# RMSNorm over 16384 rows: row scales on ScalarE, gamma from PSUM in bulk on VectorE, part of the rows on GpSimd, third tile stored in halves, gamma loaded in five pieces

## Chip, cores, metric

One core of one Trainium2 chip. The metric is device time of one execution in microseconds (us), median over runs. The kernel before takes 161.9 us (three runs, 161.73 to 162.24).

In the lines of the profile DVE is VectorE, ACT ScalarE, POOL GpSimd, PE TensorE, and SP the engine that issues the transfers of x; SPq is SP's queue of such issues. L101 is line 101 of the kernel file of that run. SBUF and PSUM are the two on-chip memories; a tile called slot lies in SBUF. A queue "runs dry" when all transfers issued so far are done. The "slack" of a store is the time by which its first byte could move before the transfers ahead of it are through.

## The reference

```python
def reference(x, gamma):                    # x: 16 x 1024 x 512 f32, gamma: 512 f32
    rms = np.sqrt(np.mean(x ** 2, axis=-1, keepdims=True) + 1e-5)
    return (x / rms * gamma).astype(np.float32)
```

33.5 MB come in and 33.5 MB go out. There is very little arithmetic for each byte.

## The kernel before

The 16384 rows are cut into four tiles of 128 partitions x 32 rows x 512. In this text a "row" is one 128x512 slice of a tile, 0.26 MB; a tile has 32 of them. There are three buffers of 64 KB per partition; tile 3 reuses the buffer of tile 0, so its load waits for tile 0's store. All transfers of x are issued by SP, in order, on one queue.

```python
load(0, 0, 0, 8)                       # tile, buffer, first row, last row
load(0, 0, 8, 32)
...
def row_stats(slot, g):                # 8 rows at a time
    if (g // G) % 2:                   # every other group: squares into PSUM, summed on VectorE
        for h in range(0, G, H):
            nc.scalar.activation(out=sq, in_=slots[slot][:, g+h : g+h+H, :], func=AF.Square)
            nc.vector.tensor_reduce(out=ss[:, h : h+H], in_=sq, axis=mybir.AxisListType.X, op=OP.add)
    else:                              # the others: ScalarE squares and sums row by row
        for r in range(G):
            nc.scalar.activation(out=sq_scratch, in_=slots[slot][:, g+r, :], func=AF.Square,
                                 accum_out=ss[:, r : r+1])
    nc.scalar.activation(out=rms, in_=ss, func=AF.Sqrt, bias=eps_t, scale=1.0 / D)
    nc.vector.reciprocal(out=rstd, in_=rms)

def apply(slot, g, rstd):              # x * rstd * gamma, one VectorE instruction per row
    for r in range(G):
        nc.vector.scalar_tensor_tensor(out=slots[slot][:, g+r, :], in0=slots[slot][:, g+r, :],
            scalar=rstd[:, r : r+1], in1=gamma_b, op0=OP.mult, op1=OP.mult)

def transfers(t, g):                   # issued by SP after apply() of group (t, g)
    if (t, g) == (0, 0):
        store(0, 0, 0, 1); load(1, 1, 0, 32); load(2, 2, 0, 16); store(0, 0, 1, 2); load(2, 2, 16, 32)
    elif (t, g) == (0, 24):
        store(0, 0, 2, 16); store(0, 0, 16, 32); load(3, 0, 0, 16); load(3, 0, 16, 32)
    elif (t, g) == (1, 24): store(1, 1, 0, 32)
    elif (t, g) == (2, 24): store(2, 2, 0, 32)
    elif (t, g) == (3, 8):  store(3, 0, 0, 16)
    elif (t, g) == (3, 24): store(3, 0, 16, 32)
```

## Time and profile before

| | before |
|---|---|
| time | 161.9 us |
| span of the profiled run | 160.4 us |
| x's DMA queue, share of 16 engines' span | 97.7% |
| busy: VectorE, ScalarE, GpSimd | 122.6, 80.1, 0.2 us |

All data go over one queue, and its transfers fill the 16 DMA engines for 97.7% of the span. The lines and their reading are in the prediction.

### The profile page before, as it was taken

The page shows a single profiled execution, that of the slowest core. Times are in us where ns is not written, and L with a number is a line of the kernel's source. Part 1 is how long each engine was busy: PE and PEld are TensorE (multiplying, and loading weights), DVE is VectorE, ACT ScalarE, POOL GpSimd, SP SyncE. Part 2 cuts the span into 40 slices and gives each one's busy share as a digit, 9 for nine tenths or more (in the row PEclk, how much of TensorE's full clock was granted, in tenths as well). Part 3 has the DMA queues.
Part 4 walks back from the last instruction along what each step waited for, and adds up shares of the span by engine and source line. Part 5 has one row for each costly group of instructions (what it writes and reads, how often), then busy time and mean ns, then how long its engine had stood idle before and what let it go on. Part 6 is the DMA issues. An engine that isn't in the chain of part 4 may idle for free.

```text
span 160.4 us, 410 instructions
## 1 busy us (share of the span) xinstructions
PE 2.0 (1%) x2; PEld 0.5 (0%) x2; DVE 122.6 (76%) x163; ACT 80.1 (50%) x162; POOL 0.2 (0%) x4
## 2 busy tenths in 40 slices
PE   4000000000000000000000000000000000000000
PEld 1000000000000000000000000000000000000000
DVE  0100928999999519999999999999999999994000
ACT  3098039990390999996900950079609940000000
POOL 0000000000000000000000000000000000000000
DMA  5999999699699999999999999998998998999993
GB/s 197 523 392 392 466 449 523 261 523 523 262 402 387 455 458 418 453 415 466 409 392 498 409 400 507 409 507 376 425 507 360 441 507 360 417 400 441 449 417 147
DMA packets 2164, 67.13 MB, mean 419 GB/s; under 512 B 241, under 2 KB 241, under 8 KB 498
## 3 DMA queue, kind: packets, MB, share of 16 engines
q1 hardware_dynamic: 2160, 67.11, 97.7%
q14 instruction: 2, 0.02, 0.0%
q10 hardware_dynamic: 2, 0.00, 0.0%
HBM read 33.56 MB, written 33.55 MB: 418 GB/s over the span
## 4 chain that ended last, share of the span: by engine, by line
DVE 67%; DMA 13%; ACT 7%; issue 2%; DVEq 0%; SPq 0%
DVE slot L88 48%; DVE ss L71 18%; DMA slot<-in_x_dram 13%; ACT sq_scratch L76 3%; ACT sq L70 3%; DVE rstd L83 1%; DVEq L154 0%; ACT rms L82 0%; SPq L42 0%
## 5 line engine op out<-in xcount | busy, mean ns | idle before, releaser
L88 DVE SCALAR_TENSOR_TENSOR slot<-slot,rstd,gamma_b 128x512 f32<-128x512 f32 x128 | 85.8, 738 | 0.1
L76 ACT ACTIVATE sq_scratch<-slot 128x512 f32<-128x512 f32 x64 | 40.0, 625 | 10.0 <-DMA slot<-in_x_dram 8.7
L70 ACT ACTIVATE sq<-slot 128x2048 f32<-128x2048 f32 x16 | 29.8, 1864 | 18.6 <-DVE ss L71 11.5
L71 DVE TENSOR_REDUCE ss<-sq 128x4 f32<-128x2048 f32 x16 | 35.9, 2274 | 3.4 <-ACT sq L70 3.4
L82 ACT ACTIVATE rms<-ss,eps_t 128x8 f32<-128x8 f32 x16 | 4.6, 297 | 25.9 <-DVE ss L71 25.7
L83 DVE RECIPROCAL rstd<-rms 128x8 f32<-128x8 f32 x16 | 3.1, 193 | 16.1 <-ACT rms L82 16.1
L76 ACT ACTIVATION_READ_ACCUMULATOR sq_scratch<-slot 128x1 f32 x64 | 11.9, 186 | 0.0
L57 DVE COPY gamma_b<-sq 128x512 f32<-128x512 f32 x1 | 0.7, 691 | 3.3 <-PE sq L55 3.3
L55 PE MATMUL sq<-gamma_row,ones_col 1*128 1x512 f32 x2 | 2.0, 1122 | 2.2 <-DMA gamma_row<-in_gamma_dram 2.2
L76 ACT ACT_TABLE_LOAD x1 | 1.3, 1283 | 1.3 <-PEq L143 1.3
L82 ACT ACT_TABLE_LOAD x1 | 1.3, 1283 | 0.0
L53 DVE MEMSET ones_col<- 1x128 f32 x1 | 0.2, 165 | 0.8 <-PEq L143 0.8
L55 PEld LDWEIGHTS sq<-gamma_row,ones_col 1*128 1x128 f32 x2 | 0.5, 306 | 2.2 <-issue 2.2
L143 POOL MEMSET const-bfloat16-1.0<- 128x1 bf16 x1 | 0.1, 101 | 0.0
L143 POOL MEMSET const-uint8-127<- 128x1 uint8 x1 | 0.1, 101 | 0.0
L143 POOL MEMSET const-float32-0.0<- 128x1 f32 x1 | 0.1, 98 | 0.2 <-issue 0.2
L143 POOL MEMSET const-float32-1.0<- 128x1 f32 x1 | 0.1, 98 | 0.0
L60 DVE MEMSET eps_t<- 128x1 f32 x1 | 0.1, 59 | 0.0
## 6 DMA issues: line engine op xcount, KB each, us to landing
slot<-in_x_dram SPq DMA_DIRECT2D x4, 4096.0 KB, 27.6
out_dram<-slot SPq DMA_DIRECT2D x3, 4096.0 KB, 18.8
slot<-in_x_dram SPq DMA_DIRECT2D x1, 6144.0 KB, 21.5
out_dram<-slot SPq DMA_DIRECT2D x1, 3584.0 KB
slot<-in_x_dram SPq DMA_DIRECT2D x1, 2048.0 KB, 7.2
out_dram<-slot SPq DMA_DIRECT2D x2, 256.0 KB, 21.3
out_dram<-slot SPq DMA_DIRECT2D x2, 29.8
gamma_row<-in_gamma_dram ACTq DMA_DIRECT2D x1, 2.0 KB
```

Source lines behind the costliest of these rows:

```text
L53: nc.vector.memset(ones_col, 1.0)
L55: nc.tensor.matmul(gamma_psum[:, 0], ones_col, gamma_row, start=True, stop=True)
L57: nc.vector.tensor_copy(out=gamma_b, in_=gamma_psum[:, 0])
L60: nc.vector.memset(eps_t, eps)
L70: nc.scalar.activation(out=sq, in_=slots[slot][:, g + h : g + h + H, :], func=AF.Square)
L71: nc.vector.tensor_reduce(out=ss[:, h : h + H], in_=sq, axis=mybir.AxisListType.X, op=OP.add)
L76: nc.scalar.activation(out=sq_scratch, in_=slots[slot][:, g + r, :], func=AF.Square, accum_out=ss[:, r : r + 1],)
L82: nc.scalar.activation(out=rms, in_=ss, func=AF.Sqrt, bias=eps_t, scale=1.0 / D)
L83: nc.vector.reciprocal(out=rstd, in_=rms)
L88: nc.vector.scalar_tensor_tensor(out=slots[slot][:, g + r, :], in0=slots[slot][:, g + r, :], scalar=rstd[:, r : r + 1], in1=gamma_b, op0=O ...
L143: nc = _bacc.Bacc("TRN2", target_bir_lowering=False, num_devices=1)
```

## The change

The change takes work off VectorE: each row was one VectorE instruction with two SBUF inputs. Now 7 or 8 rows of a group of 16 (3 at the two ends) go to GpSimd, in two passes (times the row's scale, then times gamma). ScalarE scales the others by row; VectorE multiplies these by gamma in bulk and takes gamma from PSUM. VectorE also sums the squares of all rows now. The transfers are nearly the same: tile 1's load is issued up front, tile 2 is stored in two halves, and some of the loads and stores of tiles 0 and 2 are cut smaller. The core of the diff (bookkeeping of dependences, pools and comments cut):

```diff
     load(0, 0, 0, 8)
-    load(0, 0, 8, 32)
+    load(0, 0, 8, 16)
+    load(0, 0, 16, 32)
+    load(1, 1, 0, 32)
...
-    nc.scalar.dma_start(out=gamma_row, in_=gamma.unsqueeze(0))
+    pieces = (0, 128, 224, 320, 416, D)
+    for c0, c1 in zip(pieces, pieces[1:]):
+        nc.scalar.dma_start(out=gamma_row[:, c0:c1], in_=gamma.unsqueeze(0)[:, c0:c1])
...
+    groups = [                          # tile, first row, rows, pieces squared at once, GpSimd's share
+        (0, 0, 8, (4, 4), 3), (0, 8, 8, (4, 4), 3), (0, 16, 16, (7, 5, 4), 7),
+        (1, 0, 16, (7, 5, 4), 8), (1, 16, 16, (7, 5, 4), 8), (2, 0, 16, (7, 5, 4), 8),
+        (2, 16, 16, (7, 5, 4), 7), (3, 0, 16, (7, 5, 4), 7), (3, 16, 16, (7, 5, 4), 3),
+    ]
...
+    def scale_by_pool(rstd, t, g, n, share):
+        nc.gpsimd.tensor_tensor(out=part, in0=part, in1=by_row, op=OP.mult)
+        last = nc.gpsimd.tensor_tensor(out=part, in0=part, in1=gamma_b.to_broadcast([P, share, D]), op=OP.mult)
+    def scale_rows(rstd, t, g, r0, r1):
+        for r in range(r0, r1):
+            nc.scalar.activation(out=x[:, g + r, :], in_=x[:, g + r, :], func=AF.Copy, scale=rstd[:, r])
+        scaled = nc.vector.tensor_tensor(out=part, in0=part, in1=gamma_psum.to_broadcast([P, r1 - r0, D]), op=OP.mult)
...
-        elif (t, g) == (2, 24):
-            store(2, 2, 0, 32)
+        elif (t, g) == (2, 0):
+            store(2, 2, 0, 16)
+        elif (t, g) == (2, 16):
+            store(2, 2, 16, 32)
```

The order in the loop: for group k, GpSimd's two passes are issued first, then the squares of group k+1 (12 of its 16 rows), half of group k's row scales, the rest of the squares, the other half, and at last the square root and reciprocal of group k+1.

More of the change, by code (lines that the diff above doesn't have):

```diff
@@ L27 @@
     R = 32
-    G = 8
-    H = 4
     assert N == 4 * P * R
@@ L33 @@
     ov = of.rearrange("(t p r) d -> t p r d", p=P, r=R)
+    ctx.enter_context(tc.manual_schedule())
+    nc.scalar.addr_align(128, offset=0, max_nops=0)
     const = ctx.enter_context(tc.tile_pool(name="const", bufs=1))
-    stats = ctx.enter_context(tc.tile_pool(name="stats", bufs=4))
-    psum = ctx.enter_context(tc.tile_pool(name="psum", bufs=2, space=bass.MemoryType.PSUM))
+    stats = ctx.enter_context(tc.tile_pool(name="stats", bufs=9))
+    psum = ctx.enter_context(tc.tile_pool(name="psum", bufs=1, space=bass.MemoryType.PSUM))
@@ L39 @@
     slots = [const.tile([P, R, D], fp32, name=f"slot{i}") for i in range(3)]
+    before_scale = []
     def load(t, slot, r0, r1):
-        nc.sync.dma_start(out=slots[slot][:, r0:r1], in_=xv[t][:, r0:r1])
+        dma = nc.sync.dma_start(out=slots[slot][:, r0:r1], in_=xv[t][:, r0:r1])
+        before_scale.append((slot, r0, r1, dma))
     def store(t, slot, r0, r1):
-        nc.sync.dma_start(out=ov[t][:, r0:r1], in_=slots[slot][:, r0:r1])
+        dma = nc.sync.dma_start(out=ov[t][:, r0:r1], in_=slots[slot][:, r0:r1])
+        before_scale.append((slot, r0, r1, dma))
@@ L47 @@
     load(0, 0, 0, 8)
-    load(0, 0, 8, 32)
+    load(0, 0, 8, 16)
+    load(0, 0, 16, 32)
+    load(1, 1, 0, 32)
     gamma_row = const.tile([1, D], fp32)
-    nc.scalar.dma_start(out=gamma_row, in_=gamma.unsqueeze(0))
+    pieces = (0, 128, 224, 320, 416, D)
+    for c0, c1 in zip(pieces, pieces[1:]):
+        nc.scalar.dma_start(out=gamma_row[:, c0:c1], in_=gamma.unsqueeze(0)[:, c0:c1])
     ones_col = const.tile([1, P], fp32)
-    nc.vector.memset(ones_col, 1.0)
-    gamma_psum = psum.tile([P, H, D], fp32, name="sq")
+    nc.gpsimd.memset(ones_col, 1.0)
@@ L55 @@
+    gamma_psum = psum.tile([P, 1, D], fp32, name="gamma_psum")
     nc.tensor.matmul(gamma_psum[:, 0], ones_col, gamma_row, start=True, stop=True)
-    gamma_b = const.tile([P, D], fp32)
-    nc.vector.tensor_copy(out=gamma_b, in_=gamma_psum[:, 0])
+    gamma_b = const.tile([P, 1, D], fp32)
     eps_t = const.tile([P, 1], fp32)
-    nc.vector.memset(eps_t, eps)
-    sq_scratch = const.tile([P, D], fp32)
-    def row_stats(slot, g):
-        ss = stats.tile([P, G], fp32, name="ss")
-        rms = stats.tile([P, G], fp32, name="rms")
-        rstd = stats.tile([P, G], fp32, name="rstd")
-        if (g // G) % 2:
-            for h in range(0, G, H):
-                sq = psum.tile([P, H, D], fp32, name="sq")
-                nc.scalar.activation(out=sq, in_=slots[slot][:, g + h : g + h + H, :], func=AF.Square)
-                nc.vector.tensor_reduce(
-                    out=ss[:, h : h + H], in_=sq, axis=mybir.AxisListType.X, op=OP.add
-                )
-        else:
-            for r in range(G):
-                nc.scalar.activation(
-                    out=sq_scratch,
-                    in_=slots[slot][:, g + r, :],
-                    func=AF.Square,
-                    accum_out=ss[:, r : r + 1],
-                )
-        nc.scalar.activation(out=rms, in_=ss, func=AF.Sqrt, bias=eps_t, scale=1.0 / D)
-        nc.vector.reciprocal(out=rstd, in_=rms)
-        return rstd
@@ L86, in apply @@
-    def apply(slot, g, rstd):
-        for r in range(G):
-            nc.vector.scalar_tensor_tensor(
-                out=slots[slot][:, g + r, :],
-                in0=slots[slot][:, g + r, :],
-                scalar=rstd[:, r : r + 1],
-                in1=gamma_b,
-                op0=OP.mult,
-                op1=OP.mult,
-            )
-    groups = [(t, g) for t in range(4) for g in range(0, R, G)]
-    slot_of = [0, 1, 2, 0]
+    nc.gpsimd.memset(eps_t, eps)
+    groups = [
+        (0, 0, 8, (4, 4), 3),
+        (0, 8, 8, (4, 4), 3),
+        (0, 16, 16, (7, 5, 4), 7),
+        (1, 0, 16, (7, 5, 4), 8),
+        (1, 16, 16, (7, 5, 4), 8),
+        (2, 0, 16, (7, 5, 4), 8),
+        (2, 16, 16, (7, 5, 4), 7),
+        (3, 0, 16, (7, 5, 4), 7),
+        (3, 16, 16, (7, 5, 4), 3),
+    ]
@@ new lines, with square_sums, inverse_rms @@
+    slot_of = [0, 1, 2, 0]
+    def square_sums(ss, t, g, r, m, k):
+        home, name, most = ((psum, "sq_psum", 7), (const, "sq_sbuf", 5))[k % 2]
+        sq = home.tile([P, most, D], fp32, name=name)
+        rows = slots[slot_of[t]][:, g + r : g + r + m, :]
+        nc.scalar.activation(out=sq[:, :m], in_=rows, func=AF.Square)
+        nc.vector.tensor_reduce(
+            out=ss[:, r : r + m, 0], in_=sq[:, :m], axis=mybir.AxisListType.X, op=OP.add
+        )
+    def inverse_rms(ss, n):
+        nc.scalar.activation(out=ss[:, :n, 0], in_=ss[:, :n, 0], func=AF.Sqrt, bias=eps_t, scale=1.0 / D)
+        nc.vector.reciprocal(out=ss[:, :n, 0], in_=ss[:, :n, 0])
+        return ss
@@ new lines, in scale_by_pool @@
+    def scale_by_pool(rstd, t, g, n, share):
+        part = slots[slot_of[t]][:, g + n - share : g + n, :]
+        by_row = rstd[:, n - share : n].to_broadcast([P, share, D])
+        nc.gpsimd.tensor_tensor(out=part, in0=part, in1=by_row, op=OP.mult)
+        last = nc.gpsimd.tensor_tensor(
+            out=part, in0=part, in1=gamma_b.to_broadcast([P, share, D]), op=OP.mult
+        )
+        before_scale.append((slot_of[t], g + n - share, g + n, last))
+    def scale_rows(rstd, t, g, r0, r1):
+        x = slots[slot_of[t]]
+        for r in range(r0, r1):
+            nc.scalar.activation(out=x[:, g + r, :], in_=x[:, g + r, :], func=AF.Copy, scale=rstd[:, r])
+        part = x[:, g + r0 : g + r1, :]
+        scaled = nc.vector.tensor_tensor(out=part, in0=part, in1=gamma_psum.to_broadcast([P, r1 - r0, D]), op=OP.mult)
+        for slot, b0, b1, earlier in before_scale:
+            if slot == slot_of[t] and b0 < g + r1 and g + r0 < b1:
+                tc.declare_no_dep(scaled.ins, earlier.ins, reason="ScalarE waited for it before it scaled these rows")
@@ L102, in transfers @@
             store(0, 0, 0, 1)
-            load(1, 1, 0, 32)
             load(2, 2, 0, 16)
             store(0, 0, 1, 2)
-            load(2, 2, 16, 32)
-        elif (t, g) == (0, 24):
-            store(0, 0, 2, 16)
+            load(2, 2, 16, 24)
+            store(0, 0, 2, 3)
+            load(2, 2, 24, 32)
+        elif (t, g) == (0, 16):
+            store(0, 0, 3, 16)
             store(0, 0, 16, 32)
@@ L111, in transfers, with pieces_of @@
             load(3, 0, 16, 32)
-        elif (t, g) == (1, 24):
+        elif (t, g) == (1, 16):
             store(1, 1, 0, 32)
-        elif (t, g) == (2, 24):
-            store(2, 2, 0, 32)
-        elif (t, g) == (3, 8):
+        elif (t, g) == (2, 0):
+            store(2, 2, 0, 16)
+        elif (t, g) == (2, 16):
+            store(2, 2, 16, 32)
+        elif (t, g) == (3, 0):
             store(3, 0, 0, 16)
-        elif (t, g) == (3, 24):
+        elif (t, g) == (3, 16):
             store(3, 0, 16, 32)
-    ahead = row_stats(0, 0)
-    for k, (t, g) in enumerate(groups):
-        rstd = ahead
-        if k + 1 < len(groups):
-            tn, gn = groups[k + 1]
-            ahead = row_stats(slot_of[tn], gn)
-        apply(slot_of[t], g, rstd)
+    def pieces_of(group):
+        t, g, n, pieces, share = group
+        ss = stats.tile([P, 16, 1], fp32, name="ss")
+        r = 0
+        todo = []
+        for k, m in enumerate(pieces):
+            todo.append((ss, t, g, r, m, k))
+            r += m
+        return ss, todo
+    ss, todo = pieces_of(groups[0])
+    for piece in todo:
+        square_sums(*piece)
+    rstd = inverse_rms(ss, groups[0][2])
+    nc.scalar.copy(out=gamma_b[:, 0], in_=gamma_psum[:, 0])
+    for k, group in enumerate(groups):
+        t, g, n, pieces, share = group
+        mine = n - share
+        half = (mine + 1) // 2
+        ahead = groups[k + 1 :][:1]
+        ss, todo = pieces_of(ahead[0]) if ahead else (None, [])
+        scale_by_pool(rstd, t, g, n, share)
+        for piece in todo[:2]:
+            square_sums(*piece)
+        if n < 16:
+            scale_rows(rstd, t, g, 0, mine)
+        else:
+            scale_rows(rstd, t, g, 0, half)
+        for piece in todo[2:]:
+            square_sums(*piece)
+        if n == 16:
+            scale_rows(rstd, t, g, half, mine)
         transfers(t, g)
+        for nxt in ahead:
+            rstd = inverse_rms(ss, nxt[2])
 _INS = ['x', 'gamma']
```

## The prediction

> **What bounds the kernel now.** I read the page first: the engines, the 40 slices, the DMA queues and the chain that ended last; then the issues of the SP queue and the end of DVE's timeline; then the busy time in three stretches.
>
> The page of the kernel before:
>
> ```profile
> PE 2.0 (1%) x2; PEld 0.5 (0%) x2; DVE 122.6 (76%) x163; ACT 80.1 (50%) x162; POOL 0.2 (0%) x4
> ...
> DMA  5999999699699999999999999998998998999993
> ...
> q1 hardware_dynamic: 2160, 67.11, 97.7%
> ...
> DVE 67%; DMA 13%; ACT 7%; issue 2%; DVEq 0%; SPq 0%
> ```
>
> The last line tempts one to call the kernel DVE-bound. The one above it decides otherwise: q1, which carries all loads and stores, kept the 16 DMA engines busy for 97.7% of 160.4 us, 156.7 us. The chain only says who issued the last store, not whether the DMA would have had something else to do meanwhile. The windows show the same (columns: us from the span's start, length, busy time and instructions per engine, PE clock, DMA share, GB/s):
>
> ```profile
> 1.70:20.00 18.30, 2.04 (x2) 0.50 (x2) 5.03 (x9) 8.22 (x19) 0.00 (x0) 1.00 1.01 423
> 20.00:140.00 120.00, 0.00 (x0) 0.00 (x0) 111.15 (x144) 71.43 (x143) 0.00 (x0) 1.00 1.00 431
> 140.00:159.20 19.20, 0.00 (x0) 0.00 (x0) 6.23 (x10) 0.00 (x0) 0.00 (x0) 1.00 0.93 401
> ```
>
> DMA share 1.00 at 431 GB/s for 120 us: no hole to fill. The packet records in the trace put the first descriptor of q1 at 1.74 us and the last end at 159.25, so 157.5 us carry 256 rows in and out (a row here is 128x512 f32, 0.26 MB): 0.615 us a row. What is not transfer is 1.74 us ahead and 1.15 us behind, which both kernels have.
>
> Compute runs ahead of the queue. The last issues and the last DVE work:
>
> ```profile
> 85.63 60.96 SPq L45 DMA_DIRECT2D out_dram<-slot  x4
> ...
> 136.26 9.97 DVE L88 SCALAR_TENSOR_TENSOR slot<-slot,rstd,gamma_b 128x512 f32<-128x512 f32 x15
> ```
>
> The fourth of these stores is issued when DVE ends, 146.2 us. Its 16 rows come after 240 others, so the queue needs it only at 1.74 + 240 x 0.615 = 149.4. DVE is 3 us early: that margin, not DVE's 76%, is the number to watch.
>
> **What the Trainium skill says.** "DMA: Bandwidth & Descriptors", Specifications, puts the fabric ceiling at 435 GB/s; this trace holds 431, within 1% of it, so no rearrangement of compute can gain much. "GPSIMD Engine Reference", 3.1, gives 4497 ns for an fp32 tensor_tensor of 2048 elements, twice VectorE's, and about 2.6 cycles an element; GpSimd does only four memsets in this trace, so nothing here confirms it. "SBUF — State Buffer", Who interferes with whom, says that a DVE instruction with two SBUF inputs contends with GpSimd's reads and one with a single SBUF input does not. The new DVE instructions (a reduce; a multiply by gamma in PSUM) have one SBUF input each, so I expect no blocking; no run here shows it. "ScalarE: Activation LUTs", What ACT_TABLE_LOAD costs, adds about 93 ns for each pointer operand; the row scale has one.
>
> **The change part by part.** Four durations from these groups (busy, mean ns; 128x512 and 128x2048 forms):
>
> ```profile
> L88 DVE SCALAR_TENSOR_TENSOR slot<-slot,rstd,gamma_b 128x512 f32<-128x512 f32 x128 | 85.8, 738 | 0.1
> L76 ACT ACTIVATE sq_scratch<-slot 128x512 f32<-128x512 f32 x64 | 40.0, 625 | 10.0 <-DMA slot<-in_x_dram 8.7
> L70 ACT ACTIVATE sq<-slot 128x2048 f32<-128x2048 f32 x16 | 29.8, 1864 | 18.6 <-DVE ss L71 11.5
> L71 DVE TENSOR_REDUCE ss<-sq 128x4 f32<-128x2048 f32 x16 | 35.9, 2274 | 3.4 <-ACT sq L70 3.4
> ```
>
> *Removed:* 128 DVE row operations (0.66 us start to start, 85 us) and the accumulator reads of 64 squares. All of it lay beside the DMA: worth nothing in itself.
>
> *Added, per full group of 16 rows.* ACT: squares 4 x 1.82 = 7.3, eight or nine row scales at about 0.61 (the 0.54 start to start of a row without pointer, plus an overhead I estimate from the page above) = 5, sqrt 0.3: 12.6 us. DVE: reduces 4 x 2.20 = 8.8, multiplies of 8 or 9 rows at the reduce's rate 4.4 to 5, reciprocal 0.1: about 13.6, with waits some 14.4. GpSimd: two passes over 8 rows, 16 row passes of p us each. With the page's figure p = 1.12 (estimate: 4497/4 ns), 18 us: GpSimd becomes the slowest engine.
>
> *The DMA's order.* 64 rows of loads are queued without any wait (tiles 0 and 1), then stores and loads in the same mix as before. The descriptors get smaller in a few places (8 rows instead of 24, tile 2's store in two halves): 16 KB take 0.611 us and 32 KB 1.213 in the trace, 9 ns lost per pair, with eight partitions to a DMA engine about 0.07 us for each such split, +0.25 us in all. The gamma pieces are 2 KB and are over before the first rows are squared. ACT's two extra microseconds of issues lie in the wait for the first tile, which lasts until 8 us.
>
> *When must each store be ready?* Count the rows ahead of it: tile 1's store 160, so 100.2 us; tile 2's halves 192 and 208, so 119.9 and 129.7; tile 3's halves 224 and 240, so 139.5 and 149.4. Take off about 1.2 us from issue to first byte (1.0 from the first issue at 0.73 to the first descriptor at 1.74).
>
> *When is each ready?* Tile 1 is one load and ends at about 1.74 + 64 x 0.615 = 41.1, usable at 42 (the kernel before could use it at 42.7, with one stored row ahead of it). From there DVE does seven rows of reduce after ACT's first square (42 + 3.1 + 3.8 = 49), five more (51.7), five rows of the pending multiply (54.4), four of reduce (56.6), four of multiply (58.8): the first scales of tile 1 are there at 59. Then DVE needs 14.4 us a group; the last multiply, with 13 rows, ends near 144, 4 us early. GpSimd starts tile 1 at 59.2 and, if it is slower than 14.4 us a group, never waits again. It has 8+8+8+7+7 = 38 rows, 76 row passes, before tile 3's first half may go: ready at 59.2 + 76p + 1.2, needed at 139.5. The lateness is 76p - 79.1: nothing up to p = 1.04, 2.3 us at 1.07, 4.5 at 1.10, 6 at 1.12. The other points are milder: tile 2's second half (62 row passes) holds to p = 1.12, the last half (82) to 1.08. The store of tile 2 in one piece would have needed p under 0.96: that is what its split is for.
>
> *Sum:* removed 0, +0.25 for the descriptors, perhaps -0.2 for a loading queue never touched by a wait, plus max(0, 76p - 79.1).
>
> **The rivals.** (1) *DVE was the bound, and unloading it gains time.* For it: the chain's 67%. Against it: 431 GB/s throughout, and the 3 us by which DVE's end leads. Even without any skew at the end, 67.1 MB at 435 GB/s take 154.3 us, and with 2.9 us of ends 157.2: 2% is only just inside the ideal. It would give 158.5 at best. (2) *GpSimd becomes the bound.* For it: the skill's p of 1.12, which gives 166.6 + 1.5 = 168. Against it: the shares look cut to fit: 8 rows as long as there is slack, 7 where the demand comes closest, 3 at the end, and the split store that only a p above 0.96 makes necessary. Someone who timed this would not have left 6 us on the table, when one row fewer in five groups takes ten row passes away. (3) *The DMA hides it all.* With p at or below 1.04 the span stays 160.4 to 160.8. (4) *ACT or DVE late.* At 12.6 and 14.4 us a group both have four or more microseconds; a reduce blocked by GpSimd would use that up, but its single SBUF input speaks against it.
>
> **Range and chances.** Launch and span differ by 1.5 us (161.9 to 160.4), and I keep that. Rival 3 gives 162.0, a p of 1.05 to 1.08 gives 163 to 165, the skill's p 168. The page's figure is a measurement, the shares are circumstantial evidence about a measurement I don't have; I give p up to 1.08 two chances in three. So I predict 162.5 us, 161.3 to 168.0 as the range. Faster by over 2% (under 158.7) would need the DMA to beat its own rate: 0.01. Within 2%: 0.67. Slower: 0.32.
>
> **What would show it right or wrong.** Right: q1 at 97% or more, the DMA row at 9 to the end, GpSimd at some 105 to 115 us of busy time, its passes over eight rows 8.3 us or less each, and DVE near 110. If GpSimd is the bound: passes near 9 us, back to back from 59 us to 145, waits of the SP queue for GpSimd just ahead of tile 3's first half, and a dip in the DMA row near 140 us of the size of the loss. Wrong in both: a dip before 100 us, or DVE or ACT idle behind a GpSimd pass, which would mean a shared port that I took to be free.

## The result, and the profile after

161.82 us (four runs, 161.73 to 162.15) against 162.05 us for the kernel before on the same occasion. The ratio is 0.9992, 95% interval 0.9969 to 1.0015: the same. Ratios here and below are the mean time of one kernel's fast runs over that of the other's of the same rounds, so not quite the ratio of the medians quoted.

| | before | after |
|---|---|---|
| time | 162.05 us | 161.82 us |
| span of the profiled run | 160.4 us | 159.6 us |
| x's DMA queue, share | 97.7% | 98.2% |
| busy: VectorE, ScalarE, GpSimd | 122.6, 80.1, 0.2 us | 112.9, 108.3, 108.2 us |

The page of the changed kernel, the same parts as those shown of before:

```profile
PE 2.0 (1%) x2; PEld 0.5 (0%) x2; DVE 112.9 (71%) x50; ACT 108.3 (68%) x111; POOL 108.2 (68%) x24
...
DMA  5999999969799999999999999996989999999995
...
q1 hardware_dynamic: 2736, 67.11, 98.2%
...
DVE 46%; DMA 26%; ACT 15%; DVEq 2%; issue 1%; ACTq 0%
```

VectorE's part of the chain that ended last fell from 67% to 46%, 108 us of work appeared on GpSimd, and the time did not move. The DMA row is as full as before. The same three stretches in windows (columns as in the prediction):

```profile
1.70:20.00 18.30, 2.04 (x2) 0.50 (x2) 6.30 (x4) 10.47 (x8) 3.50 (x2) 1.00 1.03 430
20.00:140.00 120.00, 0.00 (x0) 0.00 (x0) 102.14 (x46) 96.87 (x103) 102.69 (x17) 1.00 1.00 430
140.00:159.20 19.20, 0.00 (x0) 0.00 (x0) 4.42 (x2) 0.91 (x2) 1.59 (x1) 1.00 0.92 398
```

430 GB/s in the middle stretch against 431. The columns of VectorE, ScalarE and GpSimd changed; there the last two columns did not.

Which store has the least slack now is read from GpSimd's timeline (start, duration, instruction; L101 is the pass with the row's scale, L102 the pass with gamma):

```profile
59.65 7.01 POOL L101 TENSOR_TENSOR slot<-slot,ss 128x4096 f32<-128x4096 f32 x1 [6.87 <-DVE ss L95]
66.74 8.87 POOL L102 TENSOR_TENSOR slot<-slot,gamma_b 128x4096 f32<-128x4096 f32 x1
75.55 7.03 POOL L101 TENSOR_TENSOR slot<-slot,ss 128x4096 f32<-128x4096 f32 x1
...
121.34 6.17 POOL L101 TENSOR_TENSOR slot<-slot,ss 128x3584 f32<-128x3584 f32 x1
127.58 7.76 POOL L102 TENSOR_TENSOR slot<-slot,gamma_b 128x3584 f32<-128x3584 f32 x1
135.31 2.74 POOL L101 TENSOR_TENSOR slot<-slot,ss 128x1536 f32<-128x1536 f32 x1
```

The first pass of tile 1 begins at 59.65, after a wait for VectorE's reciprocal (L95). From then on no pass has a wait in brackets: each starts where the one before ends. Eight rows take 75.55 - 59.65 = 15.9 us, 1.99 us a row. Tile 3's first half (the pass at 127.58) is ready at 135.34. SP issues its store at once:

```profile
91.54 53.28 SPq L49 DMA_DIRECT2D out_dram<-slot  x5
135.37 9.45 SPq L49 DMA_DIRECT2D out_dram<-slot  x2
```

(Two answers of the SP queue's timeline: the first line merges the last five stores, the second the last two of them, the first of which is tile 3's first half, issued at 135.37.) When would the queue have run dry? The trace's packet records of x's queue run from 1.76 to 158.44 us, 0.612 us a row; 224 rows lie ahead of this store, so at 1.76 + 224 x 0.612 = 138.9. With 1.1 us from issue to first byte (an estimate from the first load, issued at 0.74, first packet at 1.76), the store is 2.5 us early. That is the least slack in the changed kernel. (1.1 us is a little high: in the run with one row more per group, below, the pass ends at 145.00 and, by the packet records, the store's first packet starts at 145.86. With 0.86 us the slack is 2.7.) VectorE's last multiply ends at 144.4, and the last store is needed at 1.76 + 240 x 0.612 = 148.6.

The kernel before had no more: its last store was issued at 146.25 and due at 149.4 (in the prediction), so with the same 1.1 us it was 2.0 us early; its third tile's store, issued at 115.83 and due at 119.9, was 3.0 us early. The change did not use up the slack, it moved the tightest point from VectorE's end to GpSimd's.

The span of the profiled run is 0.8 us shorter than that of before, since the last packet ends at 158.44 rather than 159.25; the times of the runs do not confirm it as a gain (interval of the ratio above), and the changed kernel's variants below that differ in nothing that matters have spans of 159.9 and 160.0.

### The profile page after: what moved, and what is told of

Its sections match the earlier page's. It is cut to its first block, busy times and chain, and to the rows that moved or that the text cites. A ratio compares the mean times of both kernels' runs of the same rounds, so it can differ in the third digit from the quotient of the medians.

```text
span 159.6 us, 288 instructions
## 1 busy us (share of the span) xinstructions
PE 2.0 (1%) x2; PEld 0.5 (0%) x2; DVE 112.9 (71%) x50; ACT 108.3 (68%) x111; POOL 108.2 (68%) x24
## 3 DMA queue, kind: packets, MB, share of 16 engines
q1 hardware_dynamic: 2736, 67.11, 98.2%
## 4 chain that ended last, share of the span: by engine, by line
DVE 46%; DMA 26%; ACT 15%; DVEq 2%; issue 1%; ACTq 0%
DVE ss L89 33%; DMA slot<-in_x_dram 22%; DVE slot L112 13%; ACT sq_psum L88 12%; DMA gamma_row<-in_gamma_dram 4%; ACT slot L110 2%; DVEq L201 2%; ACT ss L94 0%; ACTq L201 0%; DVE ss L95 0%; ACTq L34 0%
## 5 line engine op out<-in xcount | busy, mean ns | idle before, releaser
L101 POOL TENSOR_TENSOR slot<-slot,ss 128x1536 f32<-128x1536 f32 (+2 forms) x9 | 47.8, 5308 | 32.1 <-DVE ss L95 32.1
L89 DVE TENSOR_REDUCE ss<-sq_psum 128x4 f32<-128x2048 f32 (+1 forms) x16 | 47.8, 2988 | 24.6 <-ACT sq_psum L88 24.6
L102 POOL TENSOR_TENSOR slot<-slot,gamma_b 128x1536 f32<-128x1536 f32 (+2 forms) x9 | 60.2, 6691 | 0.7
L110 ACT ACTIVATE slot<-slot,ss 128x512 f32<-128x512 f32 x74 | 46.8, 707 | 2.0 <-DVE ss L95 2.0
L112 DVE TENSOR_TENSOR slot<-slot,gamma_psum 128x2048 f32<-128x2048 f32 (+3 forms) x16 | 41.7, 2611 | 4.9 <-ACT slot L110 4.9
L88 ACT ACTIVATE sq_psum<-slot 128x2048 f32<-128x2048 f32 (+1 forms) x16 | 38.8, 2424 | 6.2 <-DMA slot<-in_x_dram 6.2
L89 DVE TENSOR_REDUCE ss<-sq_sbuf 128x5 f32<-128x2560 f32 (+1 forms) x9 | 24.2, 2690 | 0.0
L88 ACT ACTIVATE sq_sbuf<-slot 128x2560 f32<-128x2560 f32 (+1 forms) x9 | 20.0, 2227 | 0.0
L94 ACT ACTIVATE ss<-ss,eps_t 128x16 f32<-128x16 f32 (+1 forms) x9 | 2.7, 305 | 17.0 <-DVE ss L89 17.0
L95 DVE RECIPROCAL ss<-ss 128x16 f32<-128x16 f32 (+1 forms) x9 | 2.1, 235 | 2.1 <-ACT ss L94 2.1
L64 PEld LDWEIGHTS gamma_psum<-gamma_row,ones_col 1*128 1x128 f32 x2 | 0.5, 308 | 12.2 <-issue 12.2
```

The source lines that it names most:

```text
L64: nc.tensor.matmul(gamma_psum[:, 0], ones_col, gamma_row, start=True, stop=True)
L88: nc.scalar.activation(out=sq[:, :m], in_=rows, func=AF.Square)
L89: nc.vector.tensor_reduce(out=ss[:, r : r + m, 0], in_=sq[:, :m], axis=mybir.AxisListType.X, op=OP.add)
L94: nc.scalar.activation(out=ss[:, :n, 0], in_=ss[:, :n, 0], func=AF.Sqrt, bias=eps_t, scale=1.0 / D)
L95: nc.vector.reciprocal(out=ss[:, :n, 0], in_=ss[:, :n, 0])
L101: nc.gpsimd.tensor_tensor(out=part, in0=part, in1=by_row, op=OP.mult)
```

## The experiments

The theory: the DMA queue bounds both kernels, and compute counts only by its lateness at the point where the queue has run dry. For tile 3's first half that is 59.65 + 1.99 x (GpSimd's rows from tile 1 on) + 1.1 - 138.9; with 38 rows it is -2.5 us. Rivals: VectorE's chain was the bound; or the pieces of the change cancel each other. All experiments are edits of the changed kernel; ratios are to the kernel before in the same rounds (161.9 us in the first four, 161.99 in the others).

### No arithmetic at all

```diff
-    (all from the first square_sums to the loop's end)
+    for t, g, n, pieces, share in groups:
+        transfers(t, g)
```

> The changed kernel's loads and stores in its order, with all arithmetic taken out (so the result is x itself, wrong on purpose). If the DMA queue bounds both kernels: 161.5 to 162.2 us, ratio to the kernel before 0.995 to 1.001, q1 at 98% of the span; taking away 113 us of VectorE, 108 us of ScalarE and 108 us of GpSimd gains nothing. Rival (VectorE's chain bound the kernel before): with no compute at all it falls by over 2%, under 158.7 us.

161.58 us (six runs, 161.36 to 163.43), ratio 0.999, interval 0.9954 to 1.0026. Its output is wrong, which doesn't matter for the time. The page of this run:

```profile
span 159.6 us, 83 instructions
...
PE 2.0 (1%) x2; PEld 0.5 (0%) x2; POOL 0.4 (0%) x6
...
DMA  5999999969799999999999999996989999999995
...
q1 hardware_dynamic: 2736, 67.11, 98.2%
```

With 2736 packets, 98.2% and 159.6 us it is the changed kernel to the digit, and VectorE and ScalarE are not in it. Its DMA row is the same too, so the 6s and the 7 in that row are no waits for compute. So the changed kernel stands on the floor of its own transfers, the kernel before too, within the interval (its own transfers were not run alone), and the rival that VectorE was the bound has fallen. With these transfers no division of the compute among engines can gain more than the interval leaves open, 0.5%.

### Tile 2's store in one piece again

```diff
-        elif (t, g) == (2, 0):
-            store(2, 2, 0, 16)
-        elif (t, g) == (2, 16):
-            store(2, 2, 16, 32)
+        elif (t, g) == (2, 16):
+            store(2, 2, 0, 32)
```

> The changed kernel with the third tile stored in one piece again. GpSimd finishes that tile's second half at 121.3 us in the changed kernel; with 1.1 us from issue to first byte the store's data could move from 122.4, and the queue runs dry at 1.76 + 192 x 0.612 = 119.3. My theory (a store counts only when it comes after the queue is dry): 2.5 to 3.1 us longer, 164.3 to 164.9 us, ratio 1.016 to 1.019, one dip near 120 us, GpSimd's passes at the same times. Rival (the split matters only for VectorE, or is decoration): ratio 1.000.

164.84 us (164.42 to 165.06), ratio 1.018, interval 1.0158 to 1.0201, correct. The dip is where it was expected; the stretch from 118 to 122 us in this kernel's windows:

```profile
118.00:122.00 4.00, 0.00 (x0) 0.00 (x0) 3.39 (x1) 4.00 (x5) 4.00 (x2) 1.00 0.27 115
```

and in the changed kernel's:

```profile
118.00:122.00 4.00, 0.00 (x0) 0.00 (x0) 3.10 (x1) 4.00 (x4) 4.00 (x2) 1.00 0.89 385
```

DMA share 0.27 instead of 0.89, with GpSimd busy for all 4 us in both. The loss, 3.0 us against the changed kernel, is the time between the queue run dry and the first byte after GpSimd's end. The split is not decoration: it belongs to the GpSimd shares. (In the kernel before the whole store came in time, as said above.)

### One row more for GpSimd

```diff
-        (1, 0, 16, (7, 5, 4), 8),
-        (1, 16, 16, (7, 5, 4), 8),
-        (2, 0, 16, (7, 5, 4), 8),
-        (2, 16, 16, (7, 5, 4), 7),
-        (3, 0, 16, (7, 5, 4), 7),
+        (1, 0, 16, (7, 5, 4), 9),
+        (1, 16, 16, (7, 5, 4), 9),
+        (2, 0, 16, (7, 5, 4), 9),
+        (2, 16, 16, (7, 5, 4), 8),
+        (3, 0, 16, (7, 5, 4), 8),
```

> One row more for GpSimd in each of the five groups of tiles 1, 2 and of tile 3's first half (9, 9, 9, 8, 8). Theory: a row costs 1.99 us in two passes, GpSimd starts at 59.65 and runs without a gap, so tile 3's first half is ready at 59.65 + 43 x 1.99 = 145.2, 146.3 with the issue, against 138.9 when the queue is dry: 7.4 us late, 169.2 us, ratio 1.046 (1.038 to 1.052). Rival (the DMA hides it, as it hid 8 rows): ratio 1.000. Rival (ScalarE and VectorE, relieved of five rows, gain): under 1.000.

169.14 us (168.91 to 169.24), ratio 1.0439, interval 1.0419 to 1.0458, correct. GpSimd's last long pass and the DMA in this kernel's windows:

```profile
136.11 8.89 POOL L102 TENSOR_TENSOR slot<-slot,gamma_b 128x4096 f32<-128x4096 f32 x1
```

```profile
126.00:132.00 6.00, 0.00 (x0) 0.00 (x0) 5.62 (x4) 1.83 (x4) 6.00 (x2) 1.00 0.82 350
132.00:138.00 6.00, 0.00 (x0) 0.00 (x0) 1.93 (x1) 6.00 (x11) 5.92 (x2) 1.00 1.02 437
138.00:147.00 9.00, 0.00 (x0) 0.00 (x0) 5.23 (x2) 1.72 (x3) 9.00 (x2) 1.00 0.27 117
147.00:160.00 13.00, 0.00 (x0) 0.00 (x0) 0.00 (x0) 0.00 (x0) 4.12 (x2) 1.00 1.03 444
```

The pass ends at 145.0 (145.2 expected), and from 138 to 147 us the DMA does 27% of what it could, which is 6.6 us lost, while GpSimd is busy throughout. A little is lost already at 126 to 132 us (share 0.82): the store of tile 2's second half is late too, and what it loses is part of the same total, since the lateness of tile 3's first half is counted against the undelayed queue. Five more of the 128 rows, one in each of five groups, cost 7.3 us against the changed kernel; the 2.7 us of VectorE and 3.1 us of ScalarE work that the page shows saved in all buy nothing. GpSimd has become the bound. By the sum above the cost is zero until the 2.5 us of slack are gone and 2 us for each row after that; 38 and 43 rows were run, no number between them.

### The same, with tile 1 loaded in halves

```diff
-    load(1, 1, 0, 32)
+    load(1, 1, 0, 16)
+    load(1, 1, 16, 32)
     (and 9, 9, 9, 8, 8 as above)
```

> The same one row more, and tile 1 loaded in two halves, so that its first half is there before ScalarE is ready for it. Theory: ScalarE squares tile 1 from 38.4 instead of 42.5 us, GpSimd starts tile 1 some 4.1 us earlier, at 55.6, and tile 3's first half is late by 55.6 + 85.6 + 1.1 - 138.9 = 3.4 us: 165.2 us, ratio 1.021 (1.015 to 1.027), 4 us less than with the extra row alone. Rival (GpSimd's lateness does not hang on the landing of tile 1): the same ratio as with the extra row alone, near 1.046.

165.23 us (165.11 to 165.34), ratio 1.0199, interval 1.018 to 1.0218, correct. GpSimd's first pass of tile 1 in this kernel (its lines are numbered one higher, so the scale pass is L102 here):

```profile
55.55 7.87 POOL L102 TENSOR_TENSOR slot<-slot,ss 128x4608 f32<-128x4608 f32 x1 [2.67 <-DVE ss L96]
```

It starts at 55.55 instead of 59.52, and the time is 3.9 us less. So the start of GpSimd's run hangs on the landing of tile 1, and each part of the way to the lateness has been moved by itself: the start (this one), the number of rows (the one above), and, with the undivided store, the point at which the data are due.

### Gamma from SBUF for VectorE

```diff
-        scaled = nc.vector.tensor_tensor(out=part, in0=part, in1=gamma_psum.to_broadcast([P, r1 - r0, D]), op=OP.mult)
+        scaled = nc.vector.tensor_tensor(out=part, in0=part, in1=gamma_b.to_broadcast([P, r1 - r0, D]), op=OP.mult)
```

> VectorE's bulk multiply takes gamma from its copy in SBUF instead of from PSUM, so that it has two SBUF inputs beside GpSimd's reads; nothing else changes. If the skill's contention holds as a block: two multiplies of 2.3 to 2.8 us in each group and GpSimd's passes exclude each other, GpSimd's group grows from 15.9 to about 20 us, five groups make tile 3's first half some 20 us later, 3.6 us of slack go first: 175 to 185 us, ratio 1.08 to 1.14; multiplies or passes longer in the profile. Rival (the two don't disturb each other): multiplies 2.27 us for 4 rows, passes 7.0 and 8.9, ratio 1.000.

198.55 us (198.4 to 198.67), ratio 1.2258, interval 1.2236 to 1.228, correct. The direction is that of the block, the size was underestimated. One group in this kernel's timeline:

```profile
90.15 8.82 POOL L102 TENSOR_TENSOR slot<-slot,gamma_b 128x4096 f32<-128x4096 f32 x1
...
90.57 10.55 DVE L112 TENSOR_TENSOR slot<-slot,gamma_b 128x2048 f32<-128x2048 f32 x1
101.04 2.28 DVE L89 TENSOR_REDUCE ss<-sq_psum 128x4 f32<-128x2048 f32 x1
103.24 2.27 DVE L112 TENSOR_TENSOR slot<-slot,gamma_b 128x2048 f32<-128x2048 f32 x1
...
105.76 7.02 POOL L101 TENSOR_TENSOR slot<-slot,ss 128x4096 f32<-128x4096 f32 x1 [6.79 <-DVE ss L95]
```

The multiply at 90.57 meets GpSimd's pass that began at 90.15 and takes 10.55 us instead of 2.27; it ends 2.15 us after that pass (98.97), its own length. The one at 103.24 meets no pass and takes 2.27. GpSimd's pass keeps its 8.82. So VectorE's multiply, here always the one that comes second, waits until the whole pass is over; a pass that starts during a multiply does not occur in this run. What I had not reckoned with is what the wait holds up: the reduce behind the multiply is late, so the next group's reciprocal is late, and GpSimd stands idle for 6.79 us at the next group. A group takes 105.76 - 83.05 = 22.7 us (83.05 is the start of the scale pass of the group before), where I had taken 20; a group of 7 rows takes 21.3. After five groups tile 3's first half is ready at 170.84 (VectorE's second multiply, 168.57 + 2.27) instead of 135.34, 35.5 us later; less the 2.5 us of slack, and with 3.6 us more before the last store (no packet from 181.64 to 185.26), that is 36.6 us, and 36.7 were measured. That is what PSUM does for the change. In the kernel before, every VectorE row instruction had two SBUF inputs; that GpSimd's rows would have held these up too is likely, but no run shows it.

### No rows for GpSimd

```diff
-        (0, 0, 8, (4, 4), 3), ... (3, 16, 16, (7, 5, 4), 3),
+        (0, 0, 8, (4, 4), 0), ... (3, 16, 16, (7, 5, 4), 0),
-        scale_by_pool(rstd, t, g, n, share)
+        if share:
+            scale_by_pool(rstd, t, g, n, share)
```

> GpSimd's share set to nothing; ScalarE scales all 16 rows of a group and VectorE multiplies them. Theory (ScalarE and VectorE alone are too slow for this way of working): VectorE needs 8.8 us of reduces, 8.9 of multiplies and its waits, 18 to 19 us a group against 14.4; tile 1's first scales at 63.5, the last group's at about 157, its rows done near 170, the last store ends some 11 us later: 181 to 188 us, ratio 1.12 to 1.16, VectorE busy 94 to 98% from 60 us on. Rival (GpSimd's share serves nothing, since the DMA bounds the kernel): ratio 1.000.

180.56 us (180.45 to 180.74), ratio 1.1149, interval 1.1131 to 1.1167, correct; just under the range. The stretch in which VectorE sets the pace, in this kernel's timeline (two successive groups):

```profile
81.72 0.24 DVE L95 RECIPROCAL ss<-ss 128x16 f32<-128x16 f32 x1
...
99.21 0.24 DVE L95 RECIPROCAL ss<-ss 128x16 f32<-128x16 f32 x1
```

A group takes 17.5 us: the sum of the instructions, 17.7 by my figures, without the waits that I had added. The last rows are done at 166.3 where I had said 170. So two of the change's parts, rows scaled on ScalarE and gamma in bulk on VectorE, would by themselves have cost 11%: the kernel before needs one VectorE instruction of 0.66 us a row and sums every other group's squares on ScalarE, and this way of working needs 0.55 us of reduce and 0.55 of multiply on VectorE for each row. ScalarE has no room left either: with 16 row scales it waits 0.27 us in the second of these groups, so it would set nearly the same pace. GpSimd's share is what brings the group down to 14.4 us and makes the change neutral.

### Gamma in one piece again

```diff
-    pieces = (0, 128, 224, 320, 416, D)
+    pieces = (0, D)
```

> Gamma loaded in one piece again. Theory: nothing of it lies on the path, ratio to the kernel before 0.997 to 1.001, as the changed kernel; ScalarE's four extra issues (some 2.8 us) go, the wait of the SP queue's fourth load for gamma (5.7 us in the changed kernel) goes or moves, the landing of tile 1 stays at 42.4 us. Rival (the pieces were there for time): slower than the changed kernel by more than 0.3%.

162.08 us (161.91 to 162.18), ratio 1.0005, interval 0.9992 to 1.0019, correct: no difference that can be told from the changed kernel's 0.9992. In the changed kernel the SP queue's waits show this line, and here it is gone:

```profile
SPq L45 <- DMA gamma_row<-in_gamma_dram: 5.7, 1, 5.7
```

SP's fourth load, tile 1, was held up for 5.7 us by a gamma piece. It cost nothing, since tile 1's rows are not due on the queue before 1.76 + 32 x 0.612 = 21.3 us. Why a load of x waits for gamma there, the runs do not show. One expectation missed: ScalarE is done with the issues only 0.9 us earlier (3.75 us against 4.63), not 2.8.

### GpSimd's passes in the other order

```diff
-        nc.gpsimd.tensor_tensor(out=part, in0=part, in1=by_row, op=OP.mult)
-        last = nc.gpsimd.tensor_tensor(out=part, in0=part, in1=gamma_b.to_broadcast([P, share, D]), op=OP.mult)
+        nc.gpsimd.tensor_tensor(out=part, in0=part, in1=gamma_b.to_broadcast([P, share, D]), op=OP.mult)
+        last = nc.gpsimd.tensor_tensor(out=part, in0=part, in1=by_row, op=OP.mult)
```

> GpSimd's two passes in the other order: times gamma first, then times the row's scale. Theory (the pass whose second operand is one repeated element per row is the cheap one): gamma first 8.9 us for 8 rows, scale second 7.0, ratio 1.000. Rival (the second pass is the dear one, because it follows its own writes): 7.0 first, 8.9 second. Either way the time stays, since the sum is 15.9.

161.89 us (161.74 to 162.21), ratio 0.9998, interval 0.998 to 1.0016, correct. The passes of one group in this kernel's timeline:

```profile
68.82 8.86 POOL L101 TENSOR_TENSOR slot<-slot,gamma_b 128x4096 f32<-128x4096 f32 x1
77.75 7.02 POOL L104 TENSOR_TENSOR slot<-slot,ss 128x4096 f32<-128x4096 f32 x1
```

The gamma pass takes 8.86 us as the first and 8.87 as the second; the scale pass 7.02 either way. The cost belongs to the operand, not to the place: one scale repeated along a row is read faster than gamma. Whether it is the repetition itself that does it, the runs do not separate further.

The order has a use that I had not looked for. The gamma pass need not wait for the row's scale (at tile 1 it waits for ScalarE's squares, not for the reciprocal), so GpSimd starts tile 1 at 52.90 instead of 59.65 and is done with tile 3's first half at 128.64 (122.48 + 6.16) instead of 135.34. The store is then issued at 132.81, after VectorE's multiply, instead of 135.37: the slack grows from 2.5 to 5.0 us, at no cost in time.

## Why the prediction was right

*The bound.* "DMA share 1.00 at 431 GB/s for 120 us: no hole to fill" was the step that decided the class. The run without arithmetic shows it directly: 161.58 us. The chain of waits, which gave VectorE 67%, named the engine whose work happened to end last, not the bound.

*The start of tile 1.* Worked out: first scales at 59, GpSimd at 59.2. Measured: reciprocal at 59.32, first pass at 59.65. VectorE's 14.4 us a group: 75.07 - 60.63 = 14.44 between its first reduces. Its last multiply "near 144": 144.4. ScalarE's row scale at "about 0.61": five take 3.16 us with a single one at 0.71, so 0.61 from start to start; a scale takes 0.707 us in the mean, 82 ns more than the 0.625 of a row square in the kernel before.

*The size of p.* This was the open figure. Measured p is 15.9 / 16 = 0.994 us a row pass, under the 1.04 up to which I reckoned no loss. The figure in the Trainium skill's "GPSIMD Engine Reference", 3.1, gave 1.12 (an estimate, 4497/4 ns). It was right for one of the two passes: gamma 8.86 us for 8 rows, 1.11 a row; the scale pass at 7.02 is 0.88 a row, a fifth less. So the marker "passes over eight rows 8.3 us or less each" was met only in the mean. My grounds for a smaller p, that the shares look cut to fit, turned out well, but they were no measurement, and so far it was luck; with both passes at 1.11 the same reasoning would have put the kernel at some 167 us (162.0 + 76 x 1.11 - 79.1), and the 0.32 for slower was there for that. The step after p, the lateness 76p - 79.1, is confirmed in its form by three runs: 7.3 us for five rows more (7.4 worked out), 3.4 with an earlier start (3.4), 3.0 for the undivided store (2.5 to 3.1). Its constant was 1.1 us too kind: with p = 0.994 it gives 3.6 us of slack where the trace gives 2.5, since the queue was due at 138.9 and not 139.5 and GpSimd started at 59.65 and not 59.2.

*Two slips in the sums.* "DVE is 3 us early" leaves out the time from issue to first byte, which the later sums take off; the margin that compares is 2.0 us. The best case for rival 1 is 157.2 + 1.5 = 158.7, not 158.5, so a gain of 2% (158.66) was not even just inside the ideal. Neither changes the class.

*The descriptors.* I had +0.25 us for smaller pieces. The packet records add up to 156.73 us per engine before and 156.78 after: +0.05. The packets took longer than the medians that I used, by 1.5 us per engine before and 1.3 after (the 32 KB ones before 1.223 us in the mean, not 1.213), which took back most of it. It was too small to be seen in the time.

*Gamma.* "Over before the first rows are squared" was wrong. The first squares start at 8.03 us, and the matmul that spreads gamma waited until 12.25 for the last piece; in the kernel before it ran at 2.18. It had no effect, since gamma is first used at 16.0 us (ScalarE's copy). One piece instead of five lands by 7.9.

*The rivals.* VectorE as bound: fallen with the run without arithmetic. GpSimd as bound: not in this kernel, but one row per group away. ScalarE or VectorE late: not with GpSimd's help, and by 11% without it.

## What to carry to other kernels

When the DMA engines are full, judge a change of compute by one question for each store: is it ready before the transfers ahead of it are through? Write down both times; shares of busy time and the chain of waits answer neither. Moving work to an idle engine can leave the time untouched and still put the tightest point on that engine: here 2.5 us, little more than one row, stood between no cost at all and 2 us for every further row. And check what the receiving engine shares with the one relieved: one operand moved from PSUM to SBUF made VectorE's multiplies wait for GpSimd's passes and cost 23%.

## What the Trainium skill lacked or had wrong

- "GPSIMD Engine Reference", 3.1 and 2.1: it gives 2.6 cycles an element for a two-input fp32 tensor_tensor and calls about 2.5 the floor for two inputs. The gamma pass agrees (8.86 us for 4096 elements, 2.16 ns; the page's 4497 ns for 2048 is 2.20). The pass whose second operand is one element repeated along each row took 7.02 us, 1.71 ns an element, which at the page's 1.2 GHz is 2.06 cycles: below that floor. I found no page that has this case.
- "SBUF — State Buffer", Who interferes with whom: confirmed for VectorE coming second, with the lengths of this pair of instructions, which the page lacks. With gamma in PSUM a 4-row multiply took 2.27 us beside GpSimd; with gamma in SBUF, issued 0.4 us into a GpSimd pass, 10.55 us, and the pass kept its 8.82. The page does not warn that VectorE's other work queues behind the blocked instruction, which here left GpSimd idle for 6.8 us a group.
- "DMA: Bandwidth & Descriptors", Queues, rings and completion order, says that the engines take turns between queues, but no page has a figure for a small transfer beside a full queue. Here 2 KB in five pieces landed by 12.2 us, in one piece by 7.9, behind loads of x that SP had started at 0.74; in the kernel before, issued at 0.72, they landed by 2.2. The trace agrees with the turns: the ten packets of the five pieces lie between 6.77 and 11.77 us, most of them 0.6 us apart, as long as one 16 KB packet of x takes (0.611).
